# Moving the first block's transposes, the fillers between unit products and the first weight split in a two-layer transformer kernel

## The chip, the cores and the metric

One core of one Trainium2 chip runs the kernel. The metric is device time in microseconds (us) of one execution. The kernel before takes 1290.99 us, the median of three runs (1290.98 to 1291.3). One execution was also profiled: 1291.04 us, of which 1289.3 us lie between the first and the last instruction that the profile shows.

## The reference

All is float32, 256 positions by 1024 features, two layers. Each layer adds half a gated feed-forward block (FFN), a mixer of three kinds of attention, and half a second FFN:

```
def swiglu(h, w_gate, w_up, w_down):
    a = jnp.einsum('bsd,df->bsf', h, w_gate)
    u = jnp.einsum('bsd,df->bsf', h, w_up)
    return jnp.einsum('bsf,fd->bsd', jax.nn.silu(a) * u, w_down)

for l in range(DEPTH):
    x = x + 0.5 * swiglu(rms_norm(x, ffn1_norm[l]), ffn1_w_gate[l], ffn1_w_up[l], ffn1_w_down[l])
    x = x + hybrid_mixer(rms_norm(x, mix_norm[l]), w_in[l], ...)
    x = x + 0.5 * swiglu(rms_norm(x, ffn2_norm[l]), ffn2_w_gate[l], ffn2_w_up[l], ffn2_w_down[l])
return rms_norm(x, final_norm)
```

The hidden width D_FF is 2816, which is 22 column blocks of 128. The change touches the four FFNs (in order of time f1_0, f2_0, f1_1, f2_1) and the very start of the program.

## The kernel before, in words

**Three matmuls for one.** Every float32 product is made of three fp32r matmuls. `split` (L190) gives a high part by a ScalarE copy (`high`, L185) and a low part by a VectorE subtraction (`low`, L188); `mm3` (L173) issues high by high (L176), low by high (L177) and high by low (L178). A weight matrix is brought in by an SP transfer (L344, or L322 and L331 for units), split, and used. In the profile a weight's parts are `w_h` and `w_l`, the raw weight is `w_r` (or `f_G_r`, `f_U_r` for units).

**One FFN.** `first_block` (L574) makes hidden blocks 0 and 1 row by row: for each half of the rows (t = 0, 1) a gate product (`g0`) and an up product (`u0`) into one PSUM bank, then `glu` (L559) takes silu on ScalarE (L564) and the product with the up half on VectorE (L568, the tile `f_f_b_h`). That result must be transposed on TensorE (L170, the tile `f_b0tp`), evacuated and split by ScalarE and VectorE into `f_hTh` and `f_hTl`. Before that, in the second half of the rows, `sums` (L628) puts four VectorE operations (L632 to L634) and four splits (`f_Sh`, `f_Sl`) into the queues.

The other hidden columns come in two ways. `block` (L603) makes one block of 128 columns, already transposed: a `g` and a `u` step of 24 matmuls of 256 columns each. Its PSUM bank (`x_bank`) exists once, so the `g` of block f waits until VectorE has read block f-1 (L568). `unit_product` (L655) makes one of seven products of a fast matrix multiplication: two units of 768 columns, each with seven products for gate (G) and seven for up (U), 12 matmuls of 384 columns each, in the order 1, 5, 6, 3, 7, 2, 4. The weights of products 5 and 6 need VectorE additions first (L351). `down` (L718) multiplies hidden block f by its rows of the down matrix: 12 matmuls of 512 columns, into four PSUM banks `f_a`.

**The order.** `ffn_steps` (L483) writes TensorE's order out: block 2 (`LEAD`), then after each unit product one filler from the string `FILL`: `g`, `u`, or the number of a down product. The same list orders the weight transfers and splits (`plan_ffn`, L507). The program's order on TensorE, ScalarE and VectorE is the order in which the source issues instructions. It is steered by a clock that counts estimated TensorE time (`spend`, L158): `defer(us, fn)` (L161) issues `fn` once that clock has moved on by `us`, and `need` (L165) issues what is deferred until a key is made. No real time enters it.

**The start.** `first` is the norm of f1_0: square sums, then the scaled rows (key `"rows"`), then transposes (`turn`, L456) and their split into `f_Th` and `f_Tl` (`parts_of`, L463). `load(queues[0].pop(0), 0)` at L1195 issues the first gate weights' transfer and defers their split.

Of the kernel before, what the change touches and what calls it, by code (L numbers as in the profile page):

```python
# [50 lines left out]
SEVEN = 1, 5, 6, 3, 7, 2, 4  # L51

LEAD = "gu"
FILL = "gu0 1 gu2 3 gu4 5 gu", "gu6 gu7 10 gu11 12 13 14 15"
REST = 8, 9
FIRST, SINGLE, UNIT0 = 2, 8, 10
SLOPES = [2.0 ** (-8.0 * (i + 1) / N_ALIBI) for i in range(N_ALIBI)]
# [53 lines left out]
def block_kernel(ctx: ExitStack, tc: tile.TileContext, a: dict, c: dict, out: bass.AP):  # L111
# [9 lines left out]
    def acc_bank(name):  # L121
        return ps.tile([P, 512], F32, tag="acc", name=name, bufs=4)
# [6 lines left out]
    def tp_bank(name):  # L129

        tps[0] = 0 if tps[1] else 1 - tps[0]
        if tps[0]:
            return x_bank(name).rearrange("p (a b) -> p a b", b=P)
        return ps.tile([P, 4, P], F32, tag="tp", name=name, bufs=1)
# [10 lines left out]
    def rows(t):  # L145
        return slice(t * P, (t + 1) * P)
# [14 lines left out]
    def defer(us, fn):  # L161
        clock[1] += 1
        heapq.heappush(later, (clock[0] + us, clock[1], fn))

    def need(*keys):  # L165
        while not all(k in made for k in keys):
            heapq.heappop(later)[2]()

    def transpose(o, src, n=P):
        nc.tensor.transpose(o, src, ident[:n, :n])  # L170
        spend(0.11)

    def mm3(o, st, mv, first, last, again=False):  # L173

        (sh, sl), (mh, ml) = st, mv
        nc.tensor.matmul(o, sh, mh, start=first, stop=False, skip_group_check=again)  # L176
        nc.tensor.matmul(o, sl, mh, start=False, stop=False, skip_group_check=again)  # L177
        nc.tensor.matmul(o, sh, ml, start=False, stop=last, skip_group_check=again)  # L178
        spend(3 * (max(256, o.shape[-1]) / 2400 + 0.003))
        load_some()  # L180
        while later and later[0][0] <= clock[0]:
            heapq.heappop(later)[2]()
# [7 lines left out]
    def split(hi, lo, src):  # L190
        high(hi, src)
        low(lo, src, hi)
# [191 lines left out]
    def part(*key):  # L384

        j, o, n = where[key]
        while j not in loaded:
            if queues[1] and queues[1][0][0] == j:
                assert own_open[0] and free(1, j), key
                load(queues[1].pop(0)[0], 1)  # L390
            else:
                assert free(0, queues[0][0]), key
                load(queues[0].pop(0), 0)
        hi, lo, finish, ring = loaded[j]
        finish()
        uses[j] -= 1
        return [w[:, o:o + n] for w in (hi, lo)]
# [85 lines left out]
    def ffn_steps():  # L483
# [4 lines left out]
        def others(text):  # L488
            for w in text.replace("g", " g ").replace("u", " u ").split():
                if w in single:  # L490
                    yield "B", w, single[w]
                    single[w] += 1
                else:
                    yield "D", int(w)

        steps += others(LEAD)
        for u in range(UNITS):
            fill = list(others(FILL[u]))
            for i, what in enumerate("GU"):
# [31 lines left out]
    def ffn(name, done, opening=None, opened=None):  # L531
        xTh, xTl = nT[name]
        steps, tail, f_first = ffn_steps()
        with ExitStack() as ctx2:
# [9 lines left out]
            def hidden(f, n):  # L544

                pair = [fp.tile([P, 3, S], F32R, tag=f"hT{i}", name=f"{name}_hT{i}{f}", bufs=5) for i in "hl"]
                for i in range(n):
                    hT[f + i] = [p[:, i, :] for p in pair]
                return pair
# [6 lines left out]
            def temp(nm):  # L556
                return fp.tile([P, 512], F32, tag="t", name=f"{name}_{nm}", bufs=4)

            def glu(g, u, nm, then, key):  # L559
                s, h = temp(f"{nm}_s"), temp(f"{nm}_h")  # L560
                n = g.shape[-1]

                def silu():
                    nc.scalar.activation(s[:, :n], g, AF.Silu)  # L564
                    defer(0.2 + n / 1200, times)

                def times():
                    nc.vector.tensor_tensor(h[:, :n], s[:, :n], u, op=ALU.mult)  # L568
                    made.add(key)
                    defer(0.2 + n / 960, lambda: then(h[:, :n]))  # L570

                defer(0.25, silu)

            def first_block():  # L574

                pair = hidden(0, 2)
                for t in range(NT):
                    ab = acc_bank(f"{name}_b0{t}").rearrange("p (a b) -> p a b", a=2)
                    for i in range(2):
                        for k in range(KT):  # L580
                            need((name, t, k // 4))
                            mm3(ab[:, i, :], (xTh[:, k, rows(t)], xTl[:, k, rows(t)]), part(f"{name}_{'gu'[i]}0", k),
                                k == 0, k == KT - 1)
                        if opening and t == 0 and i == 0:
                            opening()
                        if t and not i:
                            tps[1], unit_open[0] = True, True
                            sums()

                    def turn(t, h):  # L590
                        tp = tp_bank(f"{name}_b0tp{t}")
                        for k in range(2):
                            transpose(tp[:, k, :], h[:, k * P:(k + 1) * P])
                        defer(0.3, lambda: (split(pair[0][:, 0:2, rows(t)], pair[1][:, 0:2, rows(t)], tp[:, 0:2, :]),
                                            made.update((name, "hT", i, t) for i in range(2))))

                    glu(ab[:, 0, :], ab[:, 1, :], f"{name}_b0{t}", lambda h, t=t: defer(0.5, lambda: turn(t, h)), (name, "h", 0, t))
                if opening:
                    opened()

# [27 lines left out]
            def sums():  # L628
                need(*[(name, "kept", t, h) for t in range(NT) for h in range(2)])
                (a11, a12), (a21, a22) = [[kept[name, t][:, 4 * h:4 * h + 4, :] for h in range(2)] for t in range(NT)]  # L630
                tt, stt = nc.vector.tensor_tensor, nc.vector.scalar_tensor_tensor
                todo = [lambda: tt(a22, a22, a21, op=ALU.subtract), lambda: tt(a21, a11, a21, op=ALU.subtract),  # L632
                        lambda: stt(a11, a22, -1.0, a11, op0=ALU.mult, op1=ALU.subtract),
                        lambda: stt(a12, a11, -1.0, a12, op0=ALU.mult, op1=ALU.subtract)]  # L634
                todo += [lambda i=i, a=a: (split(Sh[:, i], Sl[:, i], a), made.add((name, "S", (5, 6, 7, 3)[i])))
                         for i, a in ((0, a22), (1, a11), (3, a12), (2, a21))]
                for i, fn in enumerate(todo):
                    defer(0.8 * i, fn)
# [79 lines left out]
            def down(f, t, h):  # L718
# [3 lines left out]
                mm3(acc[t][h], [p[:, rows(t)] for p in hT[f]], part(f"{name}_d{h}", f), f == f_first, f == tail[-1])  # L722

            first_block()
            for step in steps:
                if step[0] == "P":
# [464 lines left out]
    first = norm("f1_0", None, gain_cols=gain_cols)  # L1191
    first(0, 0)
    first(0, 1)
    need(("f1_0", 0, 0))
    load(queues[0].pop(0), 0)  # L1195
    need(("f1_0", 0, 1))

    def second():
        x_in(1)
# [7 lines left out]
    def opened():  # L1207
        nc.sync.dma_start(rot, c["rot"])
        nc.sync.dma_start(tab, c["tab"])
# [26 lines left out]
def build(arrays):  # L1236
    import concourse.bacc as bacc

    nc = bacc.Bacc("TRN2", target_bir_lowering=False, num_devices=1, dynamic_dma_scratch_size=SCR)
    consts = tables()  # L1240
    args = {n: nc.dram_tensor(f"in_{n}", v.shape, F32, kind="ExternalInput").ap() for n, v in arrays.items()}
    cargs = {n: nc.dram_tensor(f"c_{n}", v.shape, F32, kind="ExternalInput").ap() for n, v in consts.items()}
    o = nc.dram_tensor("out_0", (1, S, D), F32, kind="ExternalOutput").ap()
    with tile.TileContext(nc) as tc, tc.manual_schedule(engines=ORDERED):
        block_kernel(tc, args, cargs, o)
    feed = {f"in_{n}": v for n, v in arrays.items()} | {f"c_{n}": v for n, v in consts.items()}
    return nc, feed
# [9 lines left out]
```

## Time and profile before

| what | value |
|---|---|
| median of three runs | 1290.99 us |
| profiled execution | 1291.04 us |
| its span, first to last instruction | 1289.3 us |
| TensorE (PE) busy | 1257.9 us, 98% |
| VectorE (DVE) busy | 914.2 us, 71% |
| ScalarE (ACT) busy | 750.1 us, 58% |
| DMA engines, mean rate | 192 GB/s |
| chain of waits that ended last, TensorE's share | 90% |

Rows of the trace give the time from the span's start, the duration, engine, line, operation, `output<-inputs` without buffer numbers, and in brackets the idle time of that engine just before, with what ended it. Matmuls are pipelined, so start to start is a matmul's pace and its duration is longer than that.

### The profile page before, as it was taken

To read this page: it belongs to the slowest core of one execution; us is meant where nothing else is said; L and a number is where in the kernel's file an instruction comes from. 1 tells how busy PE (TensorE), PEld (TensorE's weight loads), DVE (VectorE), ACT (ScalarE), POOL (GpSimd) and SP (SyncE) were. 2 spreads that over 40 slices of the span, in tenths; PEclk is the share of its full clock that TensorE was granted. 3 is DMA by queue.
4 is the path that set the end of the run, shared out by engine and by line. 5 is a ranking of instruction groups with operands and counts; after the bars stand their busy time and mean duration, and the time that the engine had idled before them with its cause. 6 is when DMAs were issued, how large, how long until landed. Compare 5 with 4: busy or idle time off the path is not lost.

```text
span 1289.3 us, 21216 instructions
## 1 busy us (share of the span) xinstructions
PE 1257.9 (98%) x8287; PEld 1181.5 (92%) x8287; DVE 914.2 (71%) x1359; ACT 750.1 (58%) x1263; POOL 55.5 (4%) x54
## 2 busy tenths in 40 slices
PE   7899999999999999999989999999999999999997
PEld 6899988999999889999889999899999998999996
DVE  5878777765556767887687877667655577778774
ACT  5666646665556456665466566466655654655653
POOL 0000001000000000000000000000000000000000
PEclk8999999999999999999999999999999999999999
DMA  9988855545435679886488986565464467698762
GB/s 314 247 229 211 227 191 171 159 129 149 131 101 179 211 239 239 228 226 181 163 262 253 239 226 160 163 182 152 132 163 118 128 196 207 207 254 239 221 166 79
DMA packets 206308, 247.28 MB, mean 192 GB/s; under 512 B 7160, under 2 KB 190208, under 8 KB 206208
## 3 DMA queue, kind: packets, MB, share of 16 engines
q1 hardware_dynamic: 188864, 220.16, 55.1%
q0 software_dynamic: 16896, 25.17, 12.0%
q8 instruction: 65, 1.06, 0.3%
q10 hardware_dynamic: 448, 0.59, 0.1%
q14 instruction: 35, 0.29, 0.1%
HBM read 244.85 MB, written 1.05 MB: 191 GB/s over the span
## 4 chain that ended last, share of the span: by engine, by line
PE 90%; DVE 5%; ACT 1%; DMA 1%; issue 1%; POOL 0%; SPq 0%; POOLq 0%; DVEq 0%; ACTq 0%
PE f_a L178 6%; PE f_a L177 6%; PE f_a L176 6%; PE f_s L176 6%; PE f_s L178 6%; PE f_s L177 6%; PE f_b L177 5%; PE f_b L176 5%; PE f_b L178 5%; PE mx_ogate L176 4%; PE mx_ogate L178 3%; PE mx_ogate L177 3%; DVE w_l L188 2%; PE mx_odqk L176 2%; PE mx_odqk L177 2%; PE mx_odqk L178 2%
## 5 line engine op out<-in xcount | busy, mean ns | idle before, releaser
L188 DVE TENSOR_TENSOR w_l<-w_r,w_h 128x512 fp32r<-128x512 f32 (+1 forms) x484 | 386.0, 823 | 96.1 <-ACT w_h L185 94.2
L185 ACT ACTIVATE w_h<-w_r 128x512 fp32r<-128x512 f32 (+1 forms) x484 | 344.4, 734 | 94.3 <-PE f_a L177 16.9
L176 PE MATMUL f_b<-f_Th,w_h 128*128 128x256 f32 x512 | 147.3, 288 | 2.6 <-DVE f_f_b_h L568 2.6
L177 PE MATMUL f_b<-f_Th,w_l 128*128 128x256 f32 x512 | 146.8, 287 | 0.0
L178 PE MATMUL f_b<-f_Tl,w_h 128*128 128x256 f32 x512 | 146.6, 286 | 0.0
L178 PE MATMUL f_a<-w_l,f_hTh 128*128 128x512 f32 x352 | 139.9, 397 | 0.0
L176 PE MATMUL f_a<-w_h,f_hTh 128*128 128x512 f32 x352 | 139.3, 396 | 0.0
L177 PE MATMUL f_a<-w_h,f_hTl 128*128 128x512 f32 x352 | 138.8, 394 | 0.0
L188 DVE TENSOR_TENSOR w_l<-f_U_r,w_h 128x1536 fp32r<-128x1536 f32 (+1 forms) x72 | 100.1, 1399 | 32.5 <-ACT w_h L185 31.0
L185 ACT ACTIVATE w_h<-f_G_r 128x1536 fp32r<-128x1536 f32 (+1 forms) x72 | 86.2, 1199 | 54.7 <-DVE f_G_r L351 21.9
L176 PE MATMUL mx_ogate<-mx_Th,w_h 128*128 128x256 f32 x384 | 113.3, 295 | 0.0
L177 PE MATMUL mx_ogate<-mx_Th,w_l 128*128 128x256 f32 x384 | 108.8, 283 | 0.6 <-DVE w_l L188 0.6
L178 PE MATMUL mx_ogate<-mx_Tl,w_h 128*128 128x256 f32 x384 | 108.9, 283 | 0.0
L188 DVE TENSOR_TENSOR w_l<-f_G_r,w_h 128x1536 fp32r<-128x1536 f32 (+1 forms) x72 | 100.0, 1397 | 11.6 <-ACT w_h L185 11.0
L185 ACT ACTIVATE w_h<-f_U_r 128x1536 fp32r<-128x1536 f32 (+1 forms) x72 | 85.6, 1197 | 35.9 <-issue 17.4
L176 PEld LDWEIGHTS f_b<-f_Th,w_h 128*128 128x128 f32 x512 | 100.0, 195 | 3.4 <-DVE f_f_b_h L568 3.2
L178 PEld LDWEIGHTS f_b<-f_Tl,w_h 128*128 128x128 f32 x512 | 100.0, 195 | 0.0
L177 PEld LDWEIGHTS f_b<-f_Th,w_l 128*128 128x128 f32 x512 | 99.9, 195 | 0.0
L176 PE MATMUL f_s<-w_h,f_Sh 128*128 128x384 f32 x256 | 87.4, 342 | 0.0
L178 PE MATMUL f_s<-w_l,f_Sh 128*128 128x384 f32 x256 | 86.8, 339 | 0.0
L177 PE MATMUL f_s<-w_h,f_Sl 128*128 128x384 f32 x256 | 86.6, 338 | 0.0
L178 PEld LDWEIGHTS f_a<-w_l,f_hTh 128*128 128x128 f32 x352 | 66.1, 188 | 15.6
(269 smaller groups left out, 2935.4 us busy)
## 6 DMA issues: line engine op xcount, KB each, us to landing
w_r<-in_ffn_w_down SPq DMA_DIRECT2D x88, 512.0 KB, 4.3
w_r<-in_w_in SPq DMA_DIRECT2D x84, 512.0 KB, 4.0
f_G_r<-in_ffn_w_gate SPq DMA_DIRECT2D x32, 768.0 KB, 6.6
f_U_r<-in_ffn_w_up SPq DMA_DIRECT2D x32, 768.0 KB, 7.6
w_r<-in_ffn_w_gate SPq DMA_DIRECT2D x40, 512.0 KB, 5.3
w_r<-in_ffn_w_up SPq DMA_DIRECT2D x40, 512.0 KB, 5.5
f_G_r<-in_ffn_w_gate POOLq DMA_DIRECT2D x16, 768.0 KB, 8.2
f_U_r<-in_ffn_w_up POOLq DMA_DIRECT2D x16, 768.0 KB, 7.8
```

Source lines behind the costliest of these rows:

```text
L176: nc.tensor.matmul(o, sh, mh, start=first, stop=False, skip_group_check=again)
L177: nc.tensor.matmul(o, sl, mh, start=False, stop=False, skip_group_check=again)
L178: nc.tensor.matmul(o, sh, ml, start=False, stop=last, skip_group_check=again)
L185: nc.scalar.activation(hi, src, AF.Copy)
L188: nc.vector.tensor_tensor(lo, src, hi.bitcast(F32), op=ALU.subtract)
```

## The change

`FILL`'s first string has another order. The transposes of the first block are deferred by 2.5 us of the estimated clock instead of 0.5. At the start, the first weights are loaded once the scaled rows are made, not after the first half of them has been transposed and split.

```
-FILL = "gu0 1 gu2 3 gu4 5 gu", "gu6 gu7 10 gu11 12 13 14 15"
+FILL = "0 gu1 2 gu3 gu4 gu5", "gu6 gu7 10 gu11 12 13 14 15"
...
-                    glu(ab[:, 0, :], ab[:, 1, :], f"{name}_b0{t}", lambda h, t=t: defer(0.5, lambda: turn(t, h)), (name, "h", 0, t))
+                    glu(ab[:, 0, :], ab[:, 1, :], f"{name}_b0{t}", lambda h, t=t: defer(2.5, lambda: turn(t, h)), (name, "h", 0, t))
...
     first(0, 0)
     first(0, 1)
-    need(("f1_0", 0, 0))
+    need(("f1_0", 0, "rows"))
     load(queues[0].pop(0), 0)
-    need(("f1_0", 0, 1))
+    need(("f1_0", 0, 0), ("f1_0", 0, 1))
```

Written out for the first unit, with P1 to P7 for its products, the steps after block 2 were: P1 g3 P5 u3 P6 D0 P3 D1 P7 g4 P2 u4 P4 D2 for the gate side, P1 D3 P5 g5 P6 u5 P3 D4 P7 D5 P2 g6 P4 u6 for the up side, then P1 g7 of the second unit. They are now P1 D0 P5 g3 P6 u3 P3 D1 P7 D2 P2 g4 P4 u4, then P1 D3 P5 g5 P6 u5 P3 D4 P7 g6 P2 u6 P4 D5, then P1 g7. The number of instructions on TensorE, VectorE and ScalarE is the same.

TensorE in f1_0, in the g step of block 2 (`f_0_b_319`): the transposes of the first block's second half of the rows (`b0tp`).

```order
@@ -124,5 +124,4 @@
 L177 MATMUL f_0_b_319<-f_0_Th,w_l 128x256
 L178 MATMUL f_0_b_319<-f_0_Tl,w_h 128x256
-L170 MATMUL f_0_b0tp_351<-ident,f_0_f_0_b_h 128x128 x2
 L176 MATMUL f_0_b_319<-f_0_Th,w_h 128x256
 L177 MATMUL f_0_b_319<-f_0_Th,w_l 128x256
@@ -143,4 +142,5 @@
 L177 MATMUL f_0_b_319<-f_0_Th,w_l 128x256
 L178 MATMUL f_0_b_319<-f_0_Tl,w_h 128x256
+L170 MATMUL f_0_b0tp_378<-ident,f_0_f_0_b_h 128x128 x2
```

They moved down by 18 matmuls; 9 matmuls of block 2's u step stand between them and P1 now, 27 before. The transposes of the first half of the rows moved by 18 as well, and the other three FFNs show the same.

TensorE at the end of P1 (`f_0_s_142`) in f1_0, before, and then with the change:

```order
L178 MATMUL f_0_s_142<-w_l,f_0_Th 128x384
L176 MATMUL f_0_b_419<-f_0_Th,w_h 128x256
L177 MATMUL f_0_b_419<-f_0_Th,w_l 128x256
L178 MATMUL f_0_b_419<-f_0_Tl,w_h 128x256
```

```order
L178 MATMUL f_0_s_142<-w_l,f_0_Th 128x384
L176 MATMUL f_0_a_419<-w_h,f_0_hTh_144 128x512
L177 MATMUL f_0_a_419<-w_h,f_0_hTl_145 128x512
L178 MATMUL f_0_a_419<-w_l,f_0_hTh_144 128x512
```

After P1 stood the g step of block 3; now the down product of block 0 stands there, which reads the first block's `hTh` and `hTl`.

VectorE in f1_0, from the first block's L568 (second half of the rows) to block 2's, before, and then with the change:

```order
L568 TENSOR_TENSOR f_0_f_0_b_h<-f_0_f_0_b_s,f_0_b_248 128x256
L188 TENSOR_TENSOR f_0_Sl<-f_0_xr_121,f_0_Sh 128x512
L351 TENSOR_TENSOR f_0_G_1_r<-f_0_G_1_r,f_0_G_5_r 128x768
L188 TENSOR_TENSOR f_0_Sl<-f_0_xr_121,f_0_Sh 128x512
L188 TENSOR_TENSOR f_0_hTl_145<-f_0_b0tp_351,f_0_hTh_144 128x2x128
L188 TENSOR_TENSOR f_0_Sl<-f_0_xr_223,f_0_Sh 128x512
L188 TENSOR_TENSOR w_l<-f_0_G_1_r,w_h 128x768 x2
L188 TENSOR_TENSOR w_l<-w_r,w_h 128x1024
L351 TENSOR_TENSOR f_0_G_1_r<-f_0_G_1_r,f_0_G_6_r 128x768
L568 TENSOR_TENSOR f_0_f_0_b_h<-f_0_f_0_b_s,f_0_b_319 128x256
```

```order
L568 TENSOR_TENSOR f_0_f_0_b_h<-f_0_f_0_b_s,f_0_b_248 128x256
L188 TENSOR_TENSOR f_0_Sl<-f_0_xr_124,f_0_Sh 128x512
L351 TENSOR_TENSOR f_0_G_1_r<-f_0_G_1_r,f_0_G_5_r 128x768
L188 TENSOR_TENSOR f_0_Sl<-f_0_xr_124,f_0_Sh 128x512
L188 TENSOR_TENSOR f_0_Sl<-f_0_xr_223,f_0_Sh 128x512
L188 TENSOR_TENSOR w_l<-f_0_G_1_r,w_h 128x768 x2
L188 TENSOR_TENSOR f_0_hTl_145<-f_0_b0tp_378,f_0_hTh_144 128x2x128
L188 TENSOR_TENSOR w_l<-w_r,w_h 128x1024
L351 TENSOR_TENSOR f_0_G_1_r<-f_0_G_1_r,f_0_G_6_r 128x768
L568 TENSOR_TENSOR f_0_f_0_b_h<-f_0_f_0_b_s,f_0_b_319 128x256
```

The `hTl` of the second half of the rows moved behind the last `Sl` and the two `w_l` of P5's weights. On ScalarE its `hTh` moved in the same way, behind the two `w_h` of P5's weights and the `w_h` of the next single weight. Further up the queue, the first half's `hTl` stood ahead of the sums' first L632; now it stands behind them and behind the `w_l` of P1's weights.

## Rows read from the trace of the kernel before

**Rows 1.** Waits of PE, whole span: who, for what, us in total, times, longest.

```profile
PE f_b0tp L170 <- DVE f_f_b_h L568: 10.1, 4, 2.5
PE f_b L176 <- DVE f_f_b_h L568: 2.6, 2, 1.3
```

**Rows 2.** Timeline of PE: where those waits stand, and one other.

```profile
37.28 0.44 PE L170 MATMUL f_b0tp<-ident,f_f_b_h 128*128 128x128 f32 x2 [2.45 <-DVE f_f_b_h L568]
...
44.35 0.39 PE L176 MATMUL f_b<-f_Th,w_h 128*128 128x256 f32 x1 [1.32 <-DVE f_f_b_h L568]
...
481.74 0.41 PE L170 MATMUL f_b0tp<-ident,f_f_b_h 128*128 128x128 f32 x2 [2.54 <-DVE f_f_b_h L568]
...
657.31 0.63 PE L170 MATMUL f_tp<-ident,f_xs 128*128 128x128 f32 x4 [1.82 <-DVE f_xs L452]
...
670.82 0.66 PE L170 MATMUL f_b0tp<-ident,f_f_b_h 128*128 128x128 f32 x2 [2.54 <-DVE f_f_b_h L568]
...
749.72 0.39 PE L176 MATMUL f_b<-f_Th,w_h 128*128 128x256 f32 x1 [1.25 <-DVE f_f_b_h L568]
...
1114.20 0.57 PE L170 MATMUL f_b0tp<-ident,f_f_b_h 128*128 128x128 f32 x2 [2.54 <-DVE f_f_b_h L568]
```

**Rows 3.** Stretches: us, busy us and instructions of each engine, PEclk, DMA share, GB/s.

```profile
37.20:40.60 3.40, 3.32 (x28) 3.33 (x29) 3.40 (x7) 3.26 (x5) 1.45 (x1) 1.00 0.89 298
...
475.00:478.40 3.40, 3.40 (x31) 3.40 (x30) 3.37 (x4) 2.62 (x5) 0.00 (x0) 1.00 0.82 297
...
483.00:486.40 3.40, 3.40 (x18) 3.40 (x18) 3.40 (x7) 1.88 (x3) 1.33 (x1) 0.52 0.19 13
...
670.70:674.10 3.40, 3.29 (x16) 3.32 (x17) 3.40 (x6) 3.16 (x5) 1.22 (x1) 0.52 0.68 220
1114.40:1117.80 3.40, 3.40 (x18) 3.40 (x17) 3.40 (x6) 2.86 (x5) 1.33 (x1) 0.51 0.14 40
```

**Rows 4.** Timeline of PE in f2_0: the matmuls ahead of the transposes, and P6's first.

```profile
476.76 0.28 PE L178 MATMUL f_b<-f_Tl,w_h 128*128 128x256 f32 x1
...
478.92 0.28 PE L178 MATMUL f_b<-f_Tl,w_h 128*128 128x256 f32 x1
...
496.68 0.34 PE L176 MATMUL f_s<-w_h,f_Sh 128*128 128x384 f32 x1
```

**Rows 5.** Timeline of DVE in f2_0, and the first hTl of f1_1.

```profile
473.91 0.42 DVE L188 TENSOR_TENSOR f_hTl<-f_b0tp,f_hTh 128x256 fp32r<-128x256 f32 x1 [1.07 <-ACT f_hTh L185]
474.25 0.68 DVE L632 TENSOR_TENSOR f_xr<-f_xr 128x512 f32<-128x512 f32 x1
...
481.18 0.41 DVE L568 TENSOR_TENSOR f_f_b_h<-f_f_b_s,f_b 128x256 f32<-128x256 f32 x1
...
484.52 1.81 DVE L188 TENSOR_TENSOR w_l<-f_G_r,w_h 128x768 fp32r<-128x768 f32 x2
...
490.36 1.96 DVE L188 TENSOR_TENSOR w_l<-f_G_r,w_h 128x768 fp32r<-128x768 f32 x2
...
662.99 0.42 DVE L188 TENSOR_TENSOR f_hTl<-f_b0tp,f_hTh 128x256 fp32r<-128x256 f32 x1 [2.32 <-ACT f_hTh L185]
```

**Rows 6.** Timeline of ACT in f2_0: the copies of the kept rows.

```profile
472.29 1.07 ACT L475 ACTIVATE f_xr<-f_tp 128x512 f32<-128x512 f32 x2
```

**Rows 7.** Timeline of the start, PE and DVE.

```profile
11.46 0.38 PE L176 MATMUL f_b<-w_h,f_Th 128*128 128x256 f32 x1 [1.53 <-ACT w_h L185]
11.53 0.68 DVE L188 TENSOR_TENSOR w_l<-w_r,w_h 128x512 fp32r<-128x512 f32 x1
...
14.86 0.58 PE L178 MATMUL f_b<-w_l,f_Th 128*128 128x256 f32 x1 [0.94 <-DVE w_l L188]
```

**Rows 8.** A single weight of f1_0: issue on SP, time to landing (page), split on ACT.

```profile
22.66 0.37 SPq L344 DMA_DIRECT2D w_r<-in_ffn_w_up  x1
...
w_r<-in_ffn_w_up SPq DMA_DIRECT2D x40, 512.0 KB, 5.5
...
39.54 1.04 ACT L185 ACTIVATE w_h<-w_r 128x1024 fp32r<-128x1024 f32 x1
```

## The prediction

> **What bounds the kernel now.** I read the table first: TensorE is busy 98% of the span and holds 90% of the chain that ended last, so only its pauses and the pace of its matmuls can give time back. The waits of PE come next [rows 1]: two groups touch the change. `f_b0tp`, the transposes of the first block, waited 10.1 us in four places for `f_f_b_h` on VectorE; the `g` step of a single block waited 2.6 us in two places for the same line, because its only PSUM bank is read by it. The timeline of PE gives the places [rows 2]: transposes at 37.28, 481.74, 670.82 and 1114.20, one in each FFN and all for the second half of the rows; `g` steps at 44.35 (g3 in f1_0) and 749.72 (g7 in f1_1). The sixth row, 1.82 us at 657.31, is a norm's transpose, which nothing here moves. Last I read the stretches behind the long waits [rows 3]. Behind three of the four transposes the granted clock is 0.51 to 0.52, so TensorE runs at 1.2 GHz there instead of 2.4: 18 matmuls in 3.4 us where the undisturbed stretch at 475 has 31. Behind the first (37.20) it is 1.00.
>
> **The change, part by part.** I sum against the profiled execution, 1291.04 us (span 1289.3 and 1.7 around it); the median is 0.05 below, so nothing has to be converted.
>
> *Transposes later.* They move down by 18 matmuls of 256 columns. Eighteen of these take 478.92 - 476.76 = 2.16 us at full clock [rows 4]. In f2_0 TensorE stood ready at 481.74 - 2.54 = 479.20; now it comes to them at 481.36. What they wait for ended at 481.18 + 0.41 = 481.59 [rows 5], and this moves up too. VectorE's `hTl` of the first half stood ahead of the sums and held them back 1.07 us while its transposes and `hTh` were made [rows 5]. Now the first L632 starts when ScalarE's copies end, 472.29 + 1.07 = 473.36 [rows 6], plus some 0.07, instead of 474.25: 0.82 earlier. The `hTl` itself goes in behind P1's `w_l` and costs 0.34 of that (473.91 to 474.25), so `f_f_b_h` is done 0.48 earlier, at 481.11, which is 0.25 ahead of need. f2_1 repeats f2_0. In f1_1 the same `hTl` held VectorE for 2.32 us [rows 5], so more comes free there; in f1_0 the wait was 2.45 rather than 2.54. I take the four waits as gone: 2.45 + 3 x 2.54 = **10.07 us**. The first half's transposes also move by 18 matmuls; nobody waited for them, and their `hTl` is needed only in D0, microseconds later: 0.
>
> *The clock.* With those waits gone, I expect the three half-clock stretches behind them to go. Each has 18 matmuls where 31 fit at full clock [rows 3]; the 13 missing ones at 0.12 are 1.56 us, and 3.4 us at 0.48 missing would be 1.63; an instruction overlaps each edge, so I take 1.5: 3 x 1.5 = **4.5 us**. The bounds are 0 (they come anyway) and 4.9.
>
> *Fillers.* g3 stood right behind P1 and now has D0 and P5 ahead of it; g7 stood one product behind u6 and now has P4, D5 and P1 between. Each gains a product and a filler, 2.16 + 2.88 = 5 us of TensorE work by the paces below. In f1_0 P1 ended at 44.35 - 1.32 = 43.03; it now ends 2.45 earlier and g3 comes 5.04 behind it, at 45.6, while what it waited for was done at 44.3 and is no later now. So both waits go: 1.32 + 1.25 = **2.57 us** [rows 2]. No matmul is added. What is new is that D0 stands where g3 stood, and needs the `hTl` of the second half, which on VectorE moved behind a `Sl` and the two `w_l` of P5. In f2_0 these two began at 484.52 [rows 5]; without the `hTl` ahead (0.34) and with the 0.48 gained they begin at 483.70, take 1.73 to the next start and leave `hTl` done at about 485.85. TensorE: 481.36, some 0.3 for the transposes, 9 matmuls x 0.12 of u2, P1 at 12 x 0.18 (384 columns are one and a half times 256), six matmuls of D0's first half and one of the second at 0.24 (512 columns): 481.36 + 0.3 + 1.08 + 2.16 + 1.68 = 486.6. It has 0.7 to spare: 0, and if that cover goes, TensorE waits by what is missing.
>
> *What is late next.* TensorE reaches P6 earlier by 2.54 + 1.5 = 4.04; that D0 stands ahead of it in place of u3 changes nothing (12 x 0.24 against 24 x 0.12). P6's weights were done at 490.36 + 1.96 = 492.32 [rows 5] and P6 began at 496.68 [rows 4]: 4.36 us of slack, and VectorE brings 0.48 more. It holds by 0.8. Behind P6 TensorE needs 2.16 + 2.88 = 5 us for a product and a filler, and VectorE for their `w_l` 1.73 and, by size, two thirds of that, some 2.9, so the lead grows again.
>
> *First weights.* The split of the first two pieces moves ahead of `f_Th` on ScalarE; the order on VectorE stays. The first matmul waited 1.53 us for `w_h` and started at 11.46 [rows 7]; it could start some 0.5 earlier. Its triple, however, needs `w_l`, done at 11.53 + 0.68 = 12.2, and the next wait, 0.94 us up to 14.86, is again for VectorE's `w_l` [rows 7]. So 0, with 0.5 as the upper bound.
>
> *Order of transfers.* D0's weights are fetched two places earlier, g3's and u3's one place later, on SP; they are the same 512 KB each. The transfer in g3's new place was issued at 22.66 in f1_0, landed some 5.5 us later, and its turn on ScalarE came at 39.54 [rows 8]: 11 us of cover. POOL's queue is unchanged: 0.
>
> Sum: 10.07 + 4.5 + 2.57 = 17.1 us. The margins of 0.25, 0.7 and 0.8 recur in each FFN, and one or two may be short by a little: I leave 0.3 for that. 1291.0 - 16.8 = **1274.2 us**.
>
> **The rivals.**
>
> *The half clock stays or comes elsewhere.* Not every wait brings it: 2.45 at 37.28 did not, nor did the smaller ones, so it isn't the length of a wait alone. The 1.82 at 657.31 stays and could be followed by one. The Trainium skill (TensorE: Matmul & The Clock Gate, section What's actually happening) says that activity releases the throttle, and that the same kernel shows a varying number of slow matmuls from run to run, by where the kernel starts; by that the clock term would be chance, and the sum without it. Against it, this case's three runs lie within 0.32 us, less than one stretch's price. Without the clock term: 1291.0 - 12.6 = 1278.4 us. With one new stretch behind 657.31: 1275.7.
>
> *The wait moves to D0 or P6.* VectorE is busy throughout these stretches, 3.37 to 3.40 us of 3.40 [rows 3], so if what I count as earlier by 0.48 is not, D0 or P6 waits in f2_0, f1_1 and f2_1. At 0.8 each that is 2.4 us: 1276.6.
>
> *Nothing is done.* If `f_f_b_h` came later by as much as the transposes, the four waits and the clock would stay, and only the two `g` waits go: 1288.5. The order on VectorE speaks against it, since nothing was put ahead of that line but the `hTl`.
>
> *Slower.* In ScalarE's queue the second `hTh` now stands behind the high part of g3's weights, which waits for a transfer. If that lands late, the `hTh`, D0 and all behind it stop. It decides from the point where the landing is later than the turn by over 0.7 us, and the kernel is slower from some 4.9 us in each FFN (17.1 / 4 + 0.7); at 6 us it is 4 x 1.1 = 4.4 slower, 1295.4. The 11 us of cover in f1_0, the FFN with the busiest transfers, are against it [rows 8].
>
> **How the numbers follow.** Chances: forecast 0.70, clock 0.13, D0 or P6 0.12, nothing done 0.03, slower 0.02. The forecast alone spans 1272.6 (upper bounds of the clock and of the start: 4.9 and 0.5, nothing left over) to 1276. The range goes up to the clock rival with a microsecond of moved waits, 1279.5, and leaves out about 0.1 above and less below: 1272.5 to 1279.5. About 0.2% (2.6 us) is what a measurement of this kernel can tell from no change; the three upper cases are faster by far more, nothing done is the same, the last is slower: 0.95, 0.03, 0.02.
>
> **What would show it.** Right: in the waits of PE, `f_b0tp` under 1 us in all and no `f_b` for L568; granted clock 1.00 in the first 20 us of f2_0, f1_1 and f2_1; no PE row for `f_a` on `hTl` or P6 on `w_l` over 0.5 us; the pause before the first matmul shorter by about 0.5, the next one longer by as much. Wrong: half-clock stretches at other places, new waits of `f_a` on L188, or ScalarE waiting for a transfer in front of `hTh`.

## The result and the profile after

The changed kernel takes 1273.09 us (median of 4 runs, 1272.14 to 1275.12), the kernel before 1290.99 (4 runs beside it, 1290.65 to 1291.30). The ratio is 0.9863, with a 95% interval of 0.9846 to 0.9881: 1.4% faster, 17.9 us. The forecast was 1274.2 in a range of 1272.5 to 1279.5.

The profiled execution is the slowest of the four, 1275.12 us with a span of 1273.3, 16.0 shorter than the span before. TensorE (PE) of the page:

```profile
PE 1254.1 (98%) x8287; PEld 1178.7 (93%) x8287; DVE 913.9 (72%) x1359; ACT 748.1 (59%) x1263; POOL 55.6 (4%) x54
```

The number of matmuls is the same. PE was busy 1257.9 us before, so its idle time (span less busy) went from 31.4 to 19.2 us, 12.2 less, and its busy time fell by 3.8, most of it in matmuls that now run at full clock. These are the waits of PE after the change, the longest groups:

```profile
PE f_tp L170 <- DVE f_xs L452: 1.8, 1, 1.8
PE f_b L178 <- DVE w_l L188: 1.8, 2, 0.9
PE f_b L176 <- ACT f_Th L185: 1.5, 2, 1.0
PE f_tp L170 <- DVE f_xs L450: 1.5, 1, 1.5
PE heat L1186 <- DVE zeros L1178: 1.2, 1, 1.2
```

Both groups of [rows 1], 10.1 us of `f_b0tp` and 2.6 us of `f_b`, are gone, and no wait for L568 stands in their place. The same stretch of f2_0 as in [rows 5], VectorE (DVE):

```profile
468.99 0.42 DVE L568 TENSOR_TENSOR f_f_b_h<-f_f_b_s,f_b 128x256 f32<-128x256 f32 x1 [1.10 <-ACT f_f_b_s L564]
469.96 0.69 DVE L632 TENSOR_TENSOR f_xr<-f_xr 128x512 f32<-128x512 f32 x1 [0.56 <-ACT f_xr L475]
473.69 0.42 DVE L188 TENSOR_TENSOR f_hTl<-f_b0tp,f_hTh 128x256 fp32r<-128x256 f32 x1
477.23 0.41 DVE L568 TENSOR_TENSOR f_f_b_h<-f_f_b_s,f_b 128x256 f32<-128x256 f32 x1
480.24 1.82 DVE L188 TENSOR_TENSOR w_l<-f_G_r,w_h 128x768 fp32r<-128x768 f32 x2
481.97 0.42 DVE L188 TENSOR_TENSOR f_hTl<-f_b0tp,f_hTh 128x256 fp32r<-128x256 f32 x1
484.31 0.41 DVE L568 TENSOR_TENSOR f_f_b_h<-f_f_b_s,f_b 128x256 f32<-128x256 f32 x1
486.42 1.96 DVE L188 TENSOR_TENSOR w_l<-f_G_r,w_h 128x768 fp32r<-128x768 f32 x2
```

and what PE does with these values (timeline, the same stage):

```profile
477.65 0.28 PE L178 MATMUL f_b<-f_Tl,w_h 128*128 128x256 f32 x1
477.77 0.38 PE L170 MATMUL f_b0tp<-ident,f_f_b_h 128*128 128x128 f32 x2
...
482.80 0.39 PE L177 MATMUL f_a<-w_h,f_hTl 128*128 128x512 f32 x1
...
486.08 0.28 PE L176 MATMUL f_b<-f_Th,w_h 128*128 128x256 f32 x1
...
488.94 0.34 PE L176 MATMUL f_s<-w_h,f_Sh 128*128 128x384 f32 x1
```

The first row is the last matmul ahead of the second half's transposes; then come these transposes, D0's first use of that half's `hTl`, g3 and P6. None has a bracket: PE didn't wait at any of them. Set against the row on DVE that each needs: the transposes come 0.13 us after `f_f_b_h` (477.23 + 0.41 = 477.64), D0 0.41 after `hTl`, g3 1.36 after block 2's L568 (484.72), P6 0.56 after its `w_l` (488.38). For the transposes this is next to nothing to spare: where they did wait in f2_0, before, they started 0.15 after that row's end (481.74 against 481.59), and in the transposes alone, below, g3 went on 0.06 after its row (487.38 against 487.32). The `hTl` of the first half, at 473.69, no longer has idle time in front of it; in [rows 5] it held DVE for 1.07.

One wait that the change didn't touch has a new consequence. It is the norm's transpose of [rows 2] at 657.31, here at 649.66 (timeline of PE):

```profile
649.66 0.63 PE L170 MATMUL f_tp<-ident,f_xs 128*128 128x128 f32 x4 [1.83 <-DVE f_xs L452]
```

The stretches behind it, as in [rows 3]:

```profile
650.20:653.60 3.40, 3.40 (x18) 3.40 (x18) 2.41 (x3) 1.29 (x3) 0.00 (x0) 0.50 1.12 341
653.60:657.00 3.40, 3.40 (x30) 3.40 (x30) 2.23 (x4) 2.54 (x4) 0.00 (x0) 1.00 1.12 340
```

PE is granted half its clock there, 1.2 GHz, and full clock again behind it. From 32 us on to TensorE's last matmul, this is the only stretch of the profiled execution below full clock; before there were three, behind the transposes.

### The profile page after: what moved, and what is told of

The parts are those of the page before. It is cut to its first block, busy times and chain, and to the rows that moved or that the text cites. A ratio compares the mean times of both kernels' runs of the same rounds, so it can differ in the third digit from the quotient of the medians.

```text
span 1273.3 us, 21204 instructions
## 1 busy us (share of the span) xinstructions
PE 1254.1 (98%) x8287; PEld 1178.7 (93%) x8287; DVE 913.9 (72%) x1359; ACT 748.1 (59%) x1263; POOL 55.6 (4%) x54
## 4 chain that ended last, share of the span: by engine, by line
PE 94%; DVE 3%; ACT 1%; DMA 1%; issue 0%; POOL 0%; POOLq 0%; ACTq 0%; DVEq 0%
PE f_a L178 6%; PE f_a L177 6%; PE f_a L176 6%; PE f_s L176 6%; PE f_s L177 6%; PE f_s L178 6%; PE f_b L177 6%; PE f_b L178 6%; PE f_b L176 6%; PE mx_ogate L176 4%; PE mx_ogate L178 3%; PE mx_ogate L177 3%; PE mx_odqk L176 2%; PE mx_odqk L177 2%; PE mx_odqk L178 2%; PE mx_sbdil L846 1%
```

## The experiments

Seven kernels: three parts of the change alone or together, then three that move one number. They ran on two chips, each with its own runs of the kernel before: a median of 1291.36 (21 runs) beside the first four, 1291.01 (7) beside the last three. This is what their profiled executions say of PE; "half clock" counts the stretches at a granted clock of 0.50 later than 32 us, up to TensorE's last matmul (the start has two in each of these kernels); one twice as long as the others counts as 2. The kernel without the first-weights edit is `both`.

| kernel | median us (runs) | ratio, 95% interval | profiled: span | PE busy | PE idle | half clock |
|---|---|---|---|---|---|---|
| before | 1290.99 (4) | | 1289.3 | 1257.9 | 31.4 | 3 |
| after | 1273.09 (4) | 0.9863, 0.9846 to 0.9881 | 1273.3 | 1254.1 | 19.2 | 1 |
| transposes alone | 1291.92 (10) | 1.0003, 0.9992 to 1.0014 | 1287.7 | 1256.3 | 31.4 | 2, in one piece |
| fillers alone | 1286.63 (6) | 0.9965, 0.9954 to 0.9977 | 1282.6 | 1253.4 | 29.2 | 0 |
| both | 1272.40 (4) | 0.9855, 0.9840 to 0.9870 | 1270.7 | 1252.0 | 18.7 | 0 |
| first weights alone | 1291.07 (10) | 0.9999, 0.9989 to 1.0009 | 1290.0 | 1258.5 | 31.5 | 3 |
| defer by 1.5 | 1281.60 (4) | 0.9925, 0.9911 to 0.9940 | 1280.5 | 1256.2 | 24.3 | 2 |
| defer by 3.5 | 1275.08 (4) | 0.9877, 0.9862 to 0.9892 | 1273.2 | 1252.9 | 20.3 | 0 |
| g7 at its old place | 1274.39 (4) | 0.9868, 0.9851 to 0.9884 | 1274.5 | 1253.3 | 21.2 | 0 |

**The transposes alone.** The theory gave the transposes most of the gain; the rival was that the next reader of the same chain on VectorE takes over the wait.

```diff
-…defer(0.5, lambda: turn(t, h)), (name, "h", 0, t))
+…defer(2.5, lambda: turn(t, h)), (name, "h", 0, t))
```

> Only the 2.5 us deferral of the first block's transposes, the fillers in the old order. If the terms of the sum are independent (10.07 us of waits and 4.5 us of half clock belong to this edit alone): 1276.5 us, and no wait of f_b0tp. If VectorE's chain only lets the wait go on to the next instruction that needs it, g3 behind P1: in f2_0 g3 would be reached 4.0 us earlier, at about 485, while VectorE's L568 for block 2 ends no earlier than about 488.2; so a new wait of about 3.4 us at g3 in each later FFN (f1_0: about 3.0 in place of 1.32), half-clock stretches behind them, and a gain of only 0.5 to 0.7 us per FFN: 1288 to 1289 us.

Measured: 1291.92 (1288.33 to 1293.86) against 1291.36 before on that chip (21 runs): no difference. The waits for `f_b0tp` are gone; the first line of the waits of PE is now:

```profile
PE f_b L176 <- DVE f_f_b_h L568: 12.3, 5, 3.5
```

That is what was spared, less 0.4 (10.1 + 2.6 = 12.7 before). The place in f2_0, PE's transposes and g3, and g3 of f2_1:

```profile
480.36 0.38 PE L170 MATMUL f_b0tp<-ident,f_f_b_h 128*128 128x128 f32 x2
...
487.38 0.58 PE L176 MATMUL f_b<-f_Th,w_h 128*128 128x256 f32 x1 [3.48 <-DVE f_f_b_h L568]
...
1119.64 0.39 PE L176 MATMUL f_b<-f_Th,w_h 128*128 128x256 f32 x1 [3.46 <-DVE f_f_b_h L568]
```

and DVE's row that g3 waits for:

```profile
471.58 0.42 DVE L568 TENSOR_TENSOR f_f_b_h<-f_f_b_s,f_b 128x256 f32<-128x256 f32 x1 [1.09 <-ACT f_f_b_s L564]
...
486.90 0.42 DVE L568 TENSOR_TENSOR f_f_b_h<-f_f_b_s,f_b 128x256 f32<-128x256 f32 x1
```

Count from the stage's first L568. Here block 2's L568 is done 487.32 - 471.58 = 15.74 us behind it, in the changed kernel 484.72 - 468.99 = 15.73: VectorE's chain is the same. PE is ready for g3 at 487.38 - 3.48 - 471.58 = 12.32 here, and comes to it at 486.08 - 468.99 = 17.09 in the changed kernel, where D0 and P5 stand ahead. So the transposes' wait had been g3's cover. Without it and without other work in its place the wait moves one consumer down the line. The other three: 2.52 at g3 of f1_0, 1.55 at g3 of f1_1, 1.26 at g7. So the second expectation has the mechanism, and its 3.4 fits f2_0 and f2_1 but not f1_1. Its time is missed: the median is 3 us above 1288 to 1289. The profiled run, 1289.50, is one of the faster ones; what the slower runs had more isn't shown.

The stretches about the two long waits differ. The clock fell at the first while PE still waited, and not at the second:

```profile
486.20:489.60 3.40, 2.22 (x10) 2.22 (x11) 2.92 (x5) 2.00 (x4) 0.00 (x0) 0.53 1.14 216
489.60:493.00 3.40, 3.40 (x18) 3.40 (x17) 2.54 (x3) 1.33 (x2) 1.30 (x1) 0.50 0.37 110
1119.70:1123.10 3.40, 3.40 (x27) 3.40 (x28) 2.98 (x4) 3.15 (x5) 0.00 (x0) 1.00 1.07 248
```

**The fillers alone.**

```diff
-FILL = "gu0 1 gu2 3 gu4 5 gu", "gu6 gu7 10 gu11 12 13 14 15"
+FILL = "0 gu1 2 gu3 gu4 gu5", "gu6 gu7 10 gu11 12 13 14 15"
```

> Only the new order of the fillers, transposes as before. Independent terms: the two g waits go (2.57 us), the four waits of f_b0tp (10.1 us) and the three half-clock stretches stay: 1288.4 us. If the fillers alone carried the gain (rival): under 1280 us.

Measured: 1286.63 (1284.40 to 1288.47), 4.7 us less than before, where the `g` waits are worth 2.57. Of the waits, those of `f_b` for L568 are gone and the other group stands as it was:

```profile
PE f_b0tp L170 <- DVE f_f_b_h L568: 10.1, 4, 2.5
```

In the profiled run the rest is the clock. Behind the waits in f2_0, f1_1 and f2_1, of the same length and at the same instruction as in [rows 2], the stretches are these:

```profile
481.10:484.50 3.40, 3.40 (x30) 3.40 (x31) 3.40 (x6) 3.06 (x5) 1.33 (x1) 1.00 0.02 6
668.70:672.10 3.40, 3.40 (x30) 3.40 (x30) 3.40 (x6) 3.03 (x5) 1.32 (x1) 1.00 0.54 158
1109.20:1112.60 3.40, 3.40 (x30) 3.40 (x30) 3.40 (x6) 3.01 (x5) 1.33 (x1) 1.00 0.04 11
```

30 matmuls at clock 1.00 where [rows 3] has 16 to 18 at 0.51 and 0.52. PE's busy time is 1257.9 - 1253.4 = 4.5 us less than before, about 1.5 for each of the three missing stretches. The profiled run is the fastest of the six, 1284.40; the slowest, 1288.47, is where 1291.36 - 2.57 = 1288.8 would be, with all three stretches. That the runs between them had one or two is argued from this, as only one run has a trace.

**Both, without the first weights.** The two edits above together, the start as before.

> Transposes and fillers, the first weights split as before. If the first-weights edit is worth nothing, as the sum had it: the same as the changed kernel, 1272 to 1275 us. If it carries up to 0.5 us: 1273.6 against 1273.1. If it brought something through the clock at the start, 1.5 us or more apart.

Measured: 1272.40 (1271.68 to 1273.21), as fast as the changed kernel or 0.7 faster, within the spread of either. The two edits bring 0 and 4.7 us apart and some 19 together. The 1.82 wait of the norm's transpose stands here too, at 648.59, but the stretch behind it is at full clock:

```profile
649.00:652.40 3.40, 3.40 (x31) 3.40 (x30) 2.86 (x5) 2.56 (x6) 0.00 (x0) 1.00 1.13 339
```

**The first weights alone.**

```diff
-    need(("f1_0", 0, 0))
+    need(("f1_0", 0, "rows"))
     load(queues[0].pop(0), 0)
-    need(("f1_0", 0, 1))
+    need(("f1_0", 0, 0), ("f1_0", 0, 1))
```

> Only the earlier split of the first weights. The wait of 1.53 us before the first matmul shrinks to about 1.0, but the matmul at 14.86 waits for the same low part on VectorE: 1291.0 us, within 0.5. The rival, that the start is on the path by its first matmul: 1290.5.

Measured: 1291.07 (1290.60 to 1292.10, 10 runs), ratio 0.9999, interval 0.9989 to 1.0009. The start on PE, where [rows 7] has 1.53 and then 0.94:

```profile
11.28 0.38 PE L176 MATMUL f_b<-w_h,f_Th 128*128 128x256 f32 x1 [1.01 <-ACT f_Th L185]
12.01 0.38 PE L177 MATMUL f_b<-w_h,f_Tl 128*128 128x256 f32 x1 [0.34 <-DVE f_Tl L188]
12.61 0.58 PE L178 MATMUL f_b<-w_l,f_Th 128*128 128x256 f32 x1 [0.22 <-DVE w_l L188]
...
15.20 0.58 PE L178 MATMUL f_b<-w_l,f_Th 128*128 128x256 f32 x1 [0.94 <-DVE w_l L188]
```

The first pause is 0.5 shorter and ends with another operand. The half microsecond comes back at once, in two short waits that were not there before: 0.34 for `f_Tl` and 0.22 for `w_l`. The pause of 0.94 is the same, and its matmul starts 6.02 us behind the start's first transposes in both kernels (15.20 - 9.18 here, 14.86 - 8.84 before).

**Deferring by 1.5 and by 3.5.** These ask whether 2.5 is in the middle of something. Below it the transposes should run into `f_f_b_h` again, above it D0 should wait for `hTl`.

```diff
-…defer(2.5, lambda: turn(t, h)), (name, "h", 0, t))
+…defer(1.5, lambda: turn(t, h)), (name, "h", 0, t))
```

> The changed kernel with the first block's transposes deferred by 1.5 us instead of 2.5, which puts them 9 matmuls (1.08 us) further up. If VectorE's L568 sets their time, as I read it (in the changed kernel's f2_0 it ends 0.1 us ahead of them): waits of f_b0tp of about 1.0 us in f2_0 and f2_1, 0.3 to 0.7 in the other two, some 2.5 us in all, and 1275 to 1276 us. If the deferral only had to be longer than before and the rest comes from the fillers (rival): no wait and 1273.

Measured: 1281.60 (1280.68 to 1282.26), 8.5 us slower than the changed kernel. The sign is as expected, the size isn't: the transposes wait 6.0 us instead of 2.5.

```profile
PE f_b0tp L170 <- DVE f_f_b_h L568: 6.0, 4, 2.0
```

The rows of DVE in f2_0 say why:

```profile
470.75 0.69 DVE L632 TENSOR_TENSOR f_xr<-f_xr,f_xr 128x512 f32<-128x512 f32 x1
472.62 0.42 DVE L188 TENSOR_TENSOR f_hTl<-f_b0tp,f_hTh 128x256 fp32r<-128x256 f32 x1 [1.17 <-ACT f_hTh L185]
472.96 0.68 DVE L633 SCALAR_TENSOR_TENSOR f_xr<-f_xr,f_xr 128x512 f32<-128x512 f32 x1
...
478.44 0.42 DVE L568 TENSOR_TENSOR f_f_b_h<-f_f_b_s,f_b 128x256 f32<-128x256 f32 x1
```

I had counted only how much sooner PE comes. But the same number also places the first half's `hTl` on DVE. At 1.5 it stands between the sums, and DVE waits 1.17 us for `hTh` there, so L568 came at 478.44, 1.2 later than in the changed kernel, at nearly the same start of the stage (469.05 and 468.99). Behind the two longest waits, of 1.99 each in f2_0 and f2_1, the clock was halved:

```profile
479.20:482.60 3.40, 3.40 (x19) 3.40 (x17) 3.29 (x6) 2.24 (x4) 1.33 (x1) 0.50 0.01 5
1107.20:1110.60 3.40, 3.40 (x18) 3.40 (x17) 3.29 (x6) 2.18 (x4) 1.33 (x1) 0.50 0.02 5
```

With 6.0 of waits and 2 x 1.5 of clock the changed kernel's 1273.1 becomes 1282.1, against 1281.6 measured.

```diff
-…defer(2.5, lambda: turn(t, h)), (name, "h", 0, t))
+…defer(3.5, lambda: turn(t, h)), (name, "h", 0, t))
```

> The changed kernel with the transposes deferred by 3.5 us, 9 matmuls further down, right ahead of P1. Now the second half's hTl stands behind one more w_l (1.14 us) on VectorE. If D0 is the next that is late, with 0.4 us to spare in the changed kernel's f2_0: waits of f_a on hTl of about 0.7 us in f2_0 and f2_1 and less in the others, 1.5 to 2 us in all, 1274.5 to 1275. If D0 has cover (rival): the same as the changed kernel, 1273.

Measured: 1275.08 (1274.95 to 1276.09), 2.0 slower than the changed kernel. The new line in the waits of PE:

```profile
PE f_a L177 <- DVE f_hTl L188: 1.2, 2, 0.6
```

It is 0.61 in each of f2_0 and f2_1. In f2_0:

```profile
482.13 0.39 PE L176 MATMUL f_a<-w_h,f_hTh 128*128 128x512 f32 x1
483.13 0.49 PE L177 MATMUL f_a<-w_h,f_hTl 128*128 128x512 f32 x1 [0.61 <-DVE f_hTl L188]
```

The two matmuls start 1.00 apart, where the pace is 0.23 (482.57 to 482.80 in the changed kernel), so the wait costs 0.77 and not 0.61; the two together are most of the 2.0. On VectorE the `hTl` of the second half now stands behind the 1.22 us of one more `w_l`. So the cover of D0 that the prediction counted on is real, and the wait that it feared comes when the transposes go one step further.

**g7 at its old place.**

```diff
-FILL = "0 gu1 2 gu3 gu4 gu5", "gu6 gu7 10 gu11 12 13 14 15"
+FILL = "0 gu1 2 gu3 gu4 5 gu", "gu6 gu7 10 gu11 12 13 14 15"
```

> The changed kernel with the last filler moves of the first unit undone (gu4 5 gu instead of gu4 gu5): u6 stands one product ahead of g7 again. The wait of 1.25 us in f1_1 comes back, once, and none at g3: 1274.3 us. If all of the gain of the fillers comes from D0 behind P1 (rival): 1273.1.

Measured: 1274.39 (1273.57 to 1276.26), 1.3 above the changed kernel. The wait of g7 in f1_1 is back, at 739.20, and none at g3:

```profile
PE f_b L176 <- DVE f_f_b_h L568: 1.3, 1, 1.3
```

The difference of the medians agrees with that wait, though the runs of the two overlap. The profiled run is the slowest of the four, and its start has two things that the edit doesn't touch: a wait of 1.42 for a `w_h` (0.43 in the changed kernel), and a second half-clock stretch twice as long as elsewhere, 24.6 to 31.5:

```profile
28.60:32.00 3.40, 3.40 (x20) 3.40 (x20) 3.33 (x6) 1.74 (x2) 0.00 (x0) 0.58 1.13 340
```

Against the transposes alone this kernel differs by D0 behind P1 and what follows from it up to P4, and by the first weights, which are worth nothing. That is 17.5 us (1291.92 - 1274.39, on two chips whose kernels before differ by 0.35): the small edit on which the large one depends.

## Why the prediction was right

**The transposes' waits, 10.07.** Right in the mechanism, and a little small. The second L568 of f2_0 came 477.23 - 468.99 = 8.24 us behind the first, before 8.76, so 0.52 earlier where 0.48 was predicted; it leaves PE 0.13 in place of 0.25, which is hardly a margin. All four waits are gone. Both halves' transposes moved; that the 0.52 belongs to the first half's `hTl` is borne out by the deferral by 1.5, which puts it among the sums again and loses 1.2, but no run moves the second half's alone.

The size is short because the prediction took TensorE to be ready at the end of a matmul's row, where the bracket of a wait begins. Without a wait the next matmul starts before that row ends: from 477.65 to 477.77 in the changed kernel it is 0.12, from 478.92 to 481.74 before [rows 2 and 4] it was 2.82. That wait was worth 2.70, not 2.54, and the same 0.16 or 0.17 stands at all six waits of the sum: 1.0 us in all. It is part of why TensorE comes sooner to everything behind than was reckoned.

Wrong is the name on the term. The text gave 10.07 to the transposes and 2.57 to the fillers as if they could be had apart, and the transposes alone were worth nothing. In the kernel before, g3 of f2_0 started at 488.81, 0.14 us after block 2's L568 was done (488.26 + 0.41): no wait showed there, as the 2.54 of the transposes and the half clock behind them had covered it. The prediction did follow f_f_b_h, `hTl` and P6's weights to their next consumers, and costed g3 with D0 and P5 ahead of it; it didn't ask what g3 would do without them.

**The clock, 4.5.** Three stretches went, and 1.5 us each is what the fillers alone measured (4.5 of busy time for three). In the profiled run one new stretch came behind the norm's 1.83 wait, which the prediction had as a rival's variant at 1275.7; that run took 1275.12. The idle time fell by 12.2 and the two stretches less make 3.0 of the 3.8 by which PE's busy time fell; the 0.8 left is about what the six waits' 0.16 make, as the end of the last row ahead of a wait counts as busy. In the other profiles with both edits the 1.8 wait is followed by full clock, so this is a term that comes and goes. A half-clock stretch at another place was named as a sign of being wrong, and the profiled run has it. The rival that the clock is chance was put down because three runs lay within 0.32 us; the 21 later runs of the same kernel lie within 3.06, and the fillers alone lost all three stretches with the waits in place. So a wait alone doesn't settle this term, though no stretch later than 32 us was seen other than about a wait; that it came out near 4.5 is in part luck. The Trainium skill (TensorE: Matmul & The Clock Gate, section What's actually happening) says that how many matmuls run slow differs between runs of one kernel. No run here shows that directly, as each kernel has one trace; the stretches behind equal waits of 2.54 us, half clock in the kernel before and full clock in the fillers alone, fit it.

**The fillers, 2.57.** Right: both `g` waits are gone in after and in the fillers alone, and g7's 1.26 comes back when g7 does.

**What is late next: D0 by 0.7, P6 by 0.8.** Both held, with less to spare: 0.41 and 0.56. VectorE's `hTl` was done 13.40 us behind the first L568 of f2_0, where the prediction's times give 13.43; it is TensorE that came sooner. The rival that the wait moves to one of them was near; the step to a deferral of 3.5 brings it about at D0.

**First weights, 0.** Right, by the two experiments with and without it: the pause of 1.53 became 1.01 and the time didn't move. The sign that was named, the next pause longer by as much, didn't come: that pause stayed 0.94, and the half microsecond went into two short waits ahead of it. The order of the transfers cost nothing that a trace shows in f1_0's later part. In the start of the profiled run ScalarE waited 3.23 us for block 2's gate weights and split them at 20.59; in the run before at 19.72. P1 of f1_0 starts 30.05 us behind the start's first transposes in the changed kernel and 29.14 in both; but before and the fillers alone, which have the same start, lie 0.56 apart there (31.95 and 32.51). One run each is too little to lay that on the change.

**The sum.** 1290.99 - 17.14 = 1273.85, and 1273.09 and 1272.40 were measured with both edits; the 0.3 left over for short margins wasn't needed. What remains under the sum is about a microsecond: the six waits' 0.16 are of that size, though it is also less than one stretch at half clock, and within the runs' spread. Two of the prediction's own sums are off, without consequence: with the upper bounds of 4.9 and 0.5 the forecast alone begins at 1273.0 (1291.0 - 10.07 - 4.9 - 2.57 - 0.5), not 1272.6, and 17.1 / 4 + 0.7 is 5.0, not 4.9. The slower rival, ScalarE stopped by a late transfer ahead of `hTh`, didn't come: `hTl` at 481.97 has no idle time in front of it.

## What to carry to other kernels

A wait that is removed by putting an engine's next work ahead of it is paid again at the next instruction that reads the same slow chain, unless that one gets independent work ahead of it too: walk down the chain and give each reader its lead over the writer, in us, before you count anything. Price a wait from start to start against the pace (2.82 against 0.12), not by its idle time. An edge with no wait in the profile may be 0.14 us from one, and then the wait before it is what hides it; two edits that are worth 0 and 4.7 alone can be worth 19 together, so don't drop one of a pair on the evidence of its own run. A number that moves one engine's instruction moves the follow-up on the others as well (the 1.5 case: PE earlier by a microsecond, and VectorE held for 1.17).

## What the runs showed of the hardware that I had not expected

The length of TensorE's pause doesn't decide whether the clock is halved about it. With a half-clock stretch: waits of 2.54 (three times each, before and the first weights alone), 1.83 (after), 1.99 (twice, deferral by 1.5), 3.48 (the transposes alone). Without one: 2.45 (before), four of 2.4 to 2.5 (the fillers alone), 3.46 and 2.52 (the transposes alone), 1.82 (both). Nor is the fall tied to the pause's end: about the wait of 3.48 the clock fell near 486.4, a microsecond before PE went on at 487.38, and in f2_0 of the kernel before it was still 1.00 from 481.80 to 482.80, behind the wait that ended at 481.74. Each stretch costs about 1.5 us; the one about the wait of 3.48 lasted some 7 us, from 486 to 493. That they come in one run of a kernel and not in the next is argued from the times, which spread: the transposes alone ranged over 5.5 us in 10 runs, the changed kernel over 3.0 in 4, the kernel before over 0.65 in the 4 runs beside it and 3.1 in the 21 beside the first four experiments. A difference of one or two microseconds in such a kernel needs more runs than its waits alone would.
